# A streaming conformer layer: weight buffers told apart by kind, sums of weights made ahead, and a changed order of FFN products

## The chip, the cores and the metric

The kernel runs on one core of one Trainium2 chip. A core has five engines that work side by side, each through its own instructions in order: TensorE (PE, matrix products, its weight loads shown apart as PEld), VectorE (DVE), ScalarE (ACT), GpSimd (POOL) and SyncE (SP), which here does nothing but ask for DMA transfers. The metric is the device time of one execution in microseconds (us), lower is better. Three runs of the kernel before took 3102.14, 3109.66 and 3117.72 us.

## The reference

One layer over 2048 prompt frames and 64 new sample frames, width 1024, all in float32. Cut to what is computed:

```python
mod = jax.nn.silu(c) @ p['w_ada'] + p['b_ada']            # w_ada 1024 x 6144
sh1, sc1, gt1, sh2, sc2, gt2 = split(mod, 6)
h = rms_norm(x, p['norm1_g']) * (1 + sc1) + sh1
z = h @ p['w_in']                                         # 1024 x 4608
glu_a, glu_b, q, k, v, g_conv, g_attn = split(z)
u = glu_a * sigmoid(glu_b)
conv_out = silu(layer_norm(causal_depthwise_conv31(u) + b_dw)) @ p['w_conv_out']   # 512 x 1024
attn_out = band_attention(rms_norm(q), rms_norm(k), v, rel_bias) @ p['w_attn_out'] # 512 x 1024
merged = sigmoid(g_conv) * conv_out + sigmoid(g_attn) * attn_out
x = x + gt1 * (merged @ p['w_o'])                         # 1024 x 1024
h2 = rms_norm(x, p['norm2_g']) * (1 + sc2) + sh2
gate, up = split(h2 @ p['w_ffn_in'], 2)                   # 1024 x 5632
x = x + gt2 * ((silu(gate) * up) @ p['w_ffn_out'])        # 2816 x 1024
```

Outputs are the new x and the conv, key and value states. There are two modulation vectors, one for the prompt and one for the sample.

## The kernel before, in words

**Precision.** Every matrix operand is split into a rounded high part and a low remainder (`hi` by an ACT copy, `lo` by a subtraction on DVE or POOL), and a product is three matmuls, hi*hi, hi*lo, lo*hi (`mm3`, line 517).

**Stages.** The 2112 frames go in four blocks through the input projections, the convolution and the attention (up to about 1242 us), whose results are kept in DRAM. Then three blocks (`CBLOCKS`, 704, 640 and 768 frames) each go through the merge (`merge`, products with `ca` weights in column tiles ct), the output projection (`wo`), the residual and second norm (`residual`), and the FFN. The FFN multiplies its 2x2 blocks of input columns and frame halves in a seven-product scheme: with h2 cut into b11, b21 (first half of the frames) and b12, b22, there are frame operands t1 to t4, and weight sums s1 to s4 of the gate and up columns. For each of the 22 column tiles f, `up` (line 1643) runs the products s2*t2, s3*t3, s1*t1, a12*b21, a11*b11, a22*t4, s4*b22 into PSUM banks y, z, x and ny, with DVE and ACT steps between them; u (`u2`) and v are copies of partial results. `down` (line 1689) multiplies the hidden part by the output weights (`fo`) every second f. For the first five f (`EARLY`) the a11 and a12 products of the next block are done before the second half of the residual is finished (lines 1722 to 1736); W.hold keeps the `up` weights back until the residual's rows are done, since the sums and those rows share one tag (`ws`, four slots).

**Weights.** `Weights` (line 216) walks one list of keys (`weight_order`). Raw weights are loaded by SP into a ring of three slots `wst`, in the order of the list; `split` makes hi and lo in a ring of five slots each (`whi`, `wlo`), and the next key is split when a slot comes free. Weights used again are stored split in DRAM and loaded from there into whi and wlo. The modulation's slabs (`mod`, 512 KB of w_ada each, raw) stand in the same list and take `whi` slots. For the first use of an `up` key, `operand` has POOL make all four sums s1 to s4 of one f at once, when a key that needs one is split, and stores them to DRAM for the later blocks.

**Order.** The program's order is written by generators that are stepped on against a model of each engine's load (`Stream`): `stream.at(t, f)` calls f once PE's modelled time reaches t, and a `yield t` holds a generator until then. `TURN_LAG` is added to the time at which the normalised q and k rows (`kn`) are turned by PE (line 841). SP issues its DMAs in order, so one that waits for its data holds those behind it.

## Time and profile before

| what | us |
|---|---|
| median of three runs | 3109.66 |
| the profiled execution, whole | 3108.83 |
| its span, first to last instruction | 3106.9 |
| PE busy | 2976.5 |
| DVE busy | 1783.5 |
| ACT busy | 1180.2 |
| POOL busy | 1021.2 |

The profile is of one execution. A row of grouped instructions gives the engine, the operation, what it writes and reads by the program's names (out<-in), shapes and count, then the busy time and the mean duration in ns, then the idle time of the engine just before, with what ended it. In a row of waits stand the waiting engine and what it writes, then what it waited for, the total, the count and the longest. In a row of time order stand the start, the duration, the engine, what it did, and in brackets the idle time before it. SPq stands for SP's queue. Line 98 is the helper through which every compute instruction is recorded, so groups are told apart by their names. The granted clock is the share of full speed at which PE ran.

### The profile page before, as it was taken

The numbers are of one execution on the slowest core, as the hardware profiler recorded it, in microseconds if no ns is written. First come the engines' busy times: TensorE is split into PE (matmuls) and PEld (weight loads), VectorE is DVE, ScalarE is ACT, GpSimd is POOL, SyncE is SP. The second block draws the span as 40 slices with busy tenths as digits, with TensorE's granted clock in tenths as the row PEclk, the third lists the DMA queues.
The fourth block names the chain that finished last, engine by engine and source line by source line (L and its number), as shares of the span: only waits on it lengthen the run. The fifth ranks groups of instructions, "written<-read, shape, count | busy, mean of one in ns | idle before, by whom it ended". The sixth has DMA issues, their size and how long they took to land. (4 is left out here: it accounts for less than half of the span.)

```text
span 3106.9 us, 44447 instructions
## 1 busy us (share of the span) xinstructions
PE 2976.5 (96%) x16403; PEld 2641.3 (85%) x16403; DVE 1783.5 (57%) x3438; ACT 1180.2 (38%) x2105; POOL 1021.2 (33%) x638
## 2 busy tenths in 40 slices
PE   7999889999999999999999999999999999999999
PEld 4789767887788788898888897889999988999998
DVE  5798677777877895464333335554444555344344
ACT  3324432452245257354333342443333244332331
POOL 1201210111011102328767773434445342343331
PEclk9999999999999999999999999999999999999999
DMA  8889788887887788776445459654444965334434
GB/s 294 272 282 302 242 262 295 256 269 261 282 278 252 259 267 261 239 251 213 141 162 172 147 192 320 227 195 153 150 150 138 321 223 193 127 112 135 136 112 163
DMA packets 480238, 676.26 MB, mean 218 GB/s; under 512 B 37820, under 2 KB 316176, under 8 KB 480021
## 3 DMA queue, kind: packets, MB, share of 16 engines
q1 hardware_dynamic: 467669, 656.04, 64.4%
q10 hardware_dynamic: 12160, 17.35, 1.6%
q8 instruction: 129, 2.11, 0.3%
q14 instruction: 88, 0.72, 0.1%
q0 software_dynamic: 192, 0.04, 0.0%
HBM read 501.70 MB, written 171.61 MB: 217 GB/s over the span
## 5 line engine op out<-in xcount | busy, mean ns | idle before, releaser
L98 POOL TENSOR_TENSOR wlo<-wst,whi 128x1024 fp32r<-128x1024 f32 (+1 forms) x296 | 643.1, 2183 | 821.7 <-ACT whi L98 728.5
L98 ACT ACTIVATE whi<-wst 128x1024 fp32r<-128x1024 f32 (+1 forms) x361 | 354.1, 988 | 581.3 <-PE pd L98 235.0
L98 PE MATMUL ps<-t,whi 128*128 128x352 f32 (+2 forms) x2112 | 511.2, 326 | 22.4 <-ACT u L98 14.8
L98 PE MATMUL pd<-whi,hid 128*128 128x512 f32 (+1 forms) x1496 | 466.2, 390 | 0.0
L98 PEld LDWEIGHTS ps<-t,whi 128*128 128x128 f32 x2112 | 371.5, 190 | 28.4 <-ACT u L98 17.2
L98 PE MATMUL ps<-b,whi 128*128 128x352 f32 (+2 forms) x1584 | 387.7, 327 | 7.6 <-ACT early L98 5.8
L98 DVE SCALAR_TENSOR_TENSOR y<-u,wd,y 128x512 f32<-128x512 f32 (+1 forms) x480 | 371.2, 777 | 6.9
L98 PE MATMUL ps<-hh,whi 128*128 128x512 f32 (+2 forms) x992 | 364.4, 367 | 5.7 <-DVE part_l L98 2.6
L98 PE MATMUL ps<-hl,whi 128*128 128x512 f32 (+2 forms) x992 | 348.7, 351 | 0.0
L98 PE MATMUL ps<-hh,wlo 128*128 128x512 f32 (+2 forms) x992 | 347.5, 351 | 0.2 <-DVE wlo L98 0.2
L98 PE MATMUL ps<-t,wlo 128*128 128x352 f32 (+2 forms) x1056 | 342.6, 325 | 0.0
L98 PEld LDWEIGHTS pd<-whi,hid 128*128 128x128 f32 (+1 forms) x1496 | 276.1, 185 | 62.9 <-issue 0.2
L98 DVE TENSOR_TENSOR acc<-acc,pd 128x512 f32<-128x512 f32 (+1 forms) x272 | 186.8, 687 | 201.1 <-PE pd L98 201.1
L98 PE MATMUL pd<-wlo,hid 128*128 128x512 f32 (+1 forms) x748 | 291.7, 390 | 0.7 <-DMA wlo<-w_dfo_l 0.7
L98 PEld LDWEIGHTS ps<-b,whi 128*128 128x128 f32 x1584 | 278.6, 190 | 12.0 <-ACT early L98 7.7
L98 PE MATMUL ps<-b,wlo 128*128 128x352 f32 (+2 forms) x792 | 257.6, 325 | 0.0
L98 POOL TENSOR_TENSOR r<-t,mhalf 128x1 f32<-128x1 f32 (+3 forms) x68 | 84.4, 1242 | 472.9 <-DVE t L98 434.2
L98 PEld LDWEIGHTS ps<-hh,whi 128*128 128x128 f32 x992 | 190.7, 192 | 24.6 <-issue 5.1
L98 PEld LDWEIGHTS ps<-hh,wlo 128*128 128x128 f32 x992 | 189.4, 191 | 23.3 <-DVE wlo L98 0.5
L98 PEld LDWEIGHTS ps<-hl,whi 128*128 128x128 f32 x992 | 190.3, 192 | 16.1 <-issue 1.7
L98 PEld LDWEIGHTS ps<-t,wlo 128*128 128x128 f32 x1056 | 200.8, 190 | 0.0
L98 PE MATMUL ps<-cin,whi 128*128 128x384 f32 (+2 forms) x768 | 185.1, 327 | 7.3 <-DVE t L98 4.5
(198 smaller groups left out, 5102.0 us busy)
## 6 DMA issues: line engine op xcount, KB each, us to landing
wst<-sum_d SPq DMA_DIRECT2D x176, 256.0 KB, 2.9
whi<-w_din_h SPq DMA_DIRECT2D x72, 512.0 KB, 6.3
wlo<-w_din_l SPq DMA_DIRECT2D x72, 512.0 KB, 6.9
wst<-in_w_ffn_in SPq DMA_DIRECT2D x112, 256.0 KB, 3.3
wst<-in_w_ffn_in SPq DMA_DIRECT2D x49, 512.0 KB, 4.5
wmod<-in_w_ada SPq DMA_DIRECT2D x48, 512.0 KB, 7.4
wst<-in_w_o SPq DMA_DIRECT2D x48, 512.0 KB, 4.8
sum_d<-ws SPq DMA_DIRECT2D x88, 256.0 KB, 2.0
```

The lines of the kernel that those rows point to most:

```text
L98: return f(*args, **kw)
```

## The change

1. **Modulation.** The slabs leave the list of `Weights`. A class `Slabs` gives them four slots `wmod` of their own; the next slab is asked for when PE is done with one. The room comes from `dynamic_dma_scratch_size=1024` (it reserves less room for transfers), and the six small vector loads that POOL's queue issued go to ACT's.
2. **Raw weights.** From the merge on there are two more tags: `wfo`, two slots for raw `fo` weights, and `wup`, one more slot for all others. A slot is given back when its last user is done (`drop`), for raw FFN columns after each single sum. In `Weights.__init__` the first three raw weights are loaded and split at once.
3. **Sums.** `operand` makes sums one at a time, as many as are asked for; `presum` makes those of the next key as soon as its raw columns are modelled to have landed. Each is stored to DRAM on its own.
4. **`fi` weights** (the first five column tiles) are split in two halves, lo on POOL, not DVE.
5. **FFN order.** In `up`, a22 stands ahead of a11; for f = 0, s3 ahead of s2; v is copied from z right after s3, and the former f's second hidden half is split ahead of u's copy. The first five a11 and a12 products are interleaved over f, and more of them stand behind the last turn.
6. **Second chunk's inputs** of the first merge are loaded at its third column tile, not ahead of the merge.
7. **Last products.** Only the first tile of `down`'s last pass goes weight by weight; the others finish one half before the other starts. For the very last tile acc*gt + x1 is made ahead of the matmuls.
8. **Lags.** TURN_LAG 1500 to 2500, also added to the modulation's column steps; output stores 4000 later (`OUT_LAG`).

The diff, cut to its core:

```diff
-TURN_LAG = 1500.0
+TURN_LAG = 2500.0
+OUT_LAG = 4000.0
...
+class Slabs:
+    def fill(self):
+        while len(self.ready) < min(len(self.keys), self.freed + self.held):
+            (src,), a, b = self.source(self.keys[len(self.ready)])
+            w = self.pool.tile([P, a, b], F32, tag="wmod", name="wmod", bufs=self.held)
+            self.sync.dma_start(w, src)
+            self.ready.append(w)
...
+    def done(self):
+        self.given += 1
+        self.stream.at(self.stream.when("pe"), lambda n=self.given: self.free(n), True)
...
+        self.extra = {"wup": 1, "wfo": 2}
+        self.tags = {"fo": ("wfo",), "": ("wst", "wup")}
...
+        self.load_on("")
...
+    def last_phase(self, sum_pool, sum_d):
+        self.sum_pool, self.sum_d = sum_pool, sum_d
+        for kind, tag in (("fo", "wfo"), ("", "wup")):
+            self.room[tag] = self.extra[tag]
+            self.load_on(kind)
...
     def operand(self, f, op):
...
-        if f not in self.sums:
-            t = [self.sum_pool.tile([P, 4, P], F32, tag="ws", name="ws", bufs=4) for _ in range(4)]
...
+        made = self.sums.setdefault(f, [])
+        while len(made) < int(op[1]):
+            j = len(made)
+            t = self.sum_pool.tile([P, 4, P], F32, tag="ws", name="ws", bufs=4)
...
+            self.gps.tensor_tensor(t, x, y, e)
+            made.append(t)
+            for c in self.parts_of(f, f"s{j + 1}"):
+                self.drop(self.raws[c], "pool")
+            self.stream.at(
+                self.stream.when("pool"), lambda j=j, t=t: self.sync.dma_start(self.sum_d[f][j], t), True
+            )
+        return made[int(op[1]) - 1]
+
+    def presum(self):
+
+        i = len(self.ready)
+        if i in self.first and all(self.landed.get(j, 1e18) <= self.stream.load["pe"] for j in self.need[i]):
+            for f, op in self.keys[i][1:]:
+                if op[0] == "s":
+                    self.operand(f, op)
...
-        e, name = (self.dve, "dve") if key[0] in ("in", "qkv", "fi") or key[0] == "wo" and key[1] % 2 else (self.gps, "pool")
+        e, name = (self.dve, "dve") if key[0] in ("in", "qkv") or key[0] == "wo" and key[1] % 2 else (self.gps, "pool")
...
-            parts = [(slice(0, shape[1]), self.loaded[its[0]])]
+            n = 4 if key[0] == "fi" else shape[1]
+            parts = [(slice(j, j + n), self.loaded[its[0]][0][:, j : j + n]) for j in range(0, shape[1], n)]
...
-    ops = ["s2", "s3", "s1"] + ["a12"] * (f >= EARLY) + ["a11"] * (EARLY <= f + 1 < NF) + ["a22", "s4"]
+    ops = (["s2", "s3", "s1"] if f else ["s3", "s2", "s1"]) + ["a12"] * (f >= EARLY) + ["a22"] + ["a11"] * (EARLY <= f + 1 < NF) + ["s4"]
...
-            nc.gpsimd.dma_start(r1[o : o + a.shape[0]], a)
+            nc.scalar.dma_start(r1[o : o + a.shape[0]], a)
...
-                stream.when("dve"), lambda pa=pa, R=R, c6=c6, half=half: mod_columns(pa[:, 2 * P :], R, c6, 4 * half, 2)
+                stream.when("dve") + TURN_LAG, lambda pa=pa, R=R, c6=c6, half=half: mod_columns(pa[:, 2 * P :], R, c6, 4 * half, 2)
...
+    M = Slabs(nc.sync, wa, stream, list(mod_order()), source, 4)
+    M.fill()
...
             g = ahead.pop(0)
+            if ct == 2 and load:
+                load()
...
             step(y, "s2", "t2", f < EARLY, False)
-            u2 = piece("t1", "u2")[:, :half]
-            keep = (lambda dst: plus(dst, y, s1)) if f < EARLY else (lambda dst: copy(dst, y))
-            keep(u2)
             if late:
                 hidden(*late.pop())
-            z = bank("y")
-            step(z, "s3", "t3", True, False)
+            u2 = piece("t1", "u2")[:, :half]
+            keep = (lambda dst, ps: plus(dst, ps, s1)) if f < EARLY else copy
+            keep(u2, y)
+            if f:
+                z = bank("y")
+                step(z, "s3", "t3", True, False)
+            v = half_piece(1, "v")[:, :half]
+            keep(v, z)
             between()
             step(y, "s1", "t1", False, False)
-            v = half_piece(1, "v")[:, :half]
-            keep(v)
-            plus(v, z, v)
+            plus(v, y, v)
...
+                final = last and hi == T and i == len(tiles) - 1
+                x1 = [x1s[q // 3][:n, q % 3] for q in (2 * i, 2 * i + 1)] if last else None
+                if final:
+                    for j in range(2):
+                        dst = acc[i][:n, 512 * j : 512 * j + 512]
+                        dve.tensor_tensor(dst, dst, gt[:n, 512 * j : 512 * j + 512], ALU.mult)
+                        dve.tensor_tensor(dst, dst, x1[j], ALU.add)
...
-        for f in range(EARLY):
-            if f == EARLY - 2:
-                turns.drain()
-                W.hold = False
-                W.fill()
...
+        for step, f in ((first, 0), (first, 1), (second, 0), (first, 2), (second, 1)):
+            step(f)
+        while hs["columns"]:
+            turns.step(turns.gens[0])
+        W.hold = False
+        W.presum()
         turns.drain()
+        for step, f in ((first, 3), (first, 4), (second, 2), (second, 3), (second, 4)):
+            step(f)
+            W.fill()
...
-    nc = bacc.Bacc("TRN2", target_bir_lowering=False, num_devices=1)
+    nc = bacc.Bacc("TRN2", target_bir_lowering=False, num_devices=1, dynamic_dma_scratch_size=1024)
```

## Prediction

> **What bounds the kernel now.** I read the page first, then the mean granted clock, then busy time by stage, then who TensorE (PE) waited for, then the stretches in which its clock was halved.

> ```profile
> span 3106.9 us, 44447 instructions
> ...
> PE 2976.5 (96%) x16403; PEld 2641.3 (85%) x16403; DVE 1783.5 (57%) x3438; ACT 1180.2 (38%) x2105; POOL 1021.2 (33%) x638
> ```

> ```profile
> core 0: 3106.9 us, clock 0.987
> ```

> PE is busy for 2976.5 of 3106.9 us, so all its idle time is 130 us; a mean clock of 0.987 costs up to 0.013 x 3106.9 = 40 us more. No edit shortens a matmul, so 170 us is the ceiling. The stages share it unevenly (stretch, its length, then busy us of PE, PEld, DVE, ACT, POOL, granted clock, DMA share, GB/s):

> ```profile
> 33.40:1242.00 1208.60, 1147.25 (x6425) 965.68 (x6424) 930.23 (x1916) 494.57 (x955) 149.79 (x134) 0.98 0.84 271
> ...
> 1414.00:1884.00 470.00, 455.10 (x2470) 415.81 (x2471) 185.67 (x323) 162.44 (x305) 326.50 (x240) 0.99 0.53 180
> ...
> 2051.00:2429.00 378.00, 377.89 (x2266) 354.86 (x2264) 153.85 (x282) 131.09 (x213) 163.24 (x69) 1.00 0.48 158
> ...
> 2616.00:3100.00 484.00, 484.00 (x2531) 451.50 (x2531) 202.31 (x338) 141.48 (x219) 163.93 (x70) 1.00 0.41 133
> ```

> Projections and attention (to 1242) lose 61 us of PE. The FFN of block 0 loses 15; the FFNs of blocks 1 and 2 lose nothing, so there an edit can only cost. The waits of PE (total us, times, longest) name what could go:

> ```profile
> PE pt L98 <- DVE kn L98: 16.1, 9, 3.4
> PE ps L98 <- ACT u L98: 14.8, 8, 2.1
> ...
> PE ps L98 <- ACT t L98: 7.6, 2, 4.3
> PE ps L98 <- DMA whi<-w_dqkv_h: 7.1, 3, 2.6
> PE ps L98 <- ACT early L98: 5.8, 3, 3.3
> ...
> PE ps L98 <- DVE t L98: 4.5, 1, 4.5
> PE ps L98 <- POOL wlo L98: 3.9, 4, 1.7
> PE pa L98 <- DVE R L98: 3.5, 5, 1.0
> ...
> PE ps L98 <- DMA whi<-w_din_h: 2.4, 1, 2.4
> ```

> Behind several of them the granted clock (third number from the end) falls to a half:

> ```profile
> 408.80:415.60 6.80, 5.71 (x18) 4.66 (x18) 5.97 (x18) 1.85 (x8) 0.00 (x0) 0.50 1.01 368
> 463.40:470.20 6.80, 5.53 (x18) 4.78 (x19) 4.71 (x11) 2.40 (x6) 0.00 (x0) 0.50 1.02 402
> ...
> 1262.20:1265.50 3.30, 3.09 (x11) 3.09 (x12) 2.74 (x7) 1.52 (x3) 0.00 (x0) 0.50 0.63 189
> 1402.10:1408.90 6.80, 6.05 (x21) 6.05 (x22) 4.93 (x9) 3.73 (x9) 6.72 (x7) 0.50 0.89 302
> 1412.40:1419.10 6.70, 5.03 (x17) 5.03 (x18) 2.69 (x4) 2.20 (x4) 6.64 (x6) 0.50 0.73 240
> 1552.30:1555.70 3.40, 3.40 (x14) 3.40 (x13) 0.28 (x1) 0.64 (x2) 2.38 (x1) 0.50 0.38 154
> 1736.70:1740.00 3.30, 3.30 (x13) 3.30 (x12) 0.52 (x1) 0.46 (x1) 1.91 (x1) 0.50 0.57 230
> ...
> 2043.90:2050.60 6.70, 5.49 (x20) 5.50 (x21) 4.99 (x9) 1.68 (x3) 2.14 (x1) 0.50 0.52 157
> ```

> I price such a stretch at half its PE busy time.

> **The change part by part** (gain in us, in brackets the two ends).

> *Modulation slabs leave the ring: 11 (0 to 15.1).* Four slabs of a modulation step hold four of the five hi slots, so the next weights are asked for in one burst when they come free:

> ```profile
> 460.84 0.53 SPq L314 DMA_DIRECT2D whi<-w_dqkv_h  x1
> ...
> 466.96 0.32 SPq L314 DMA_DIRECT2D wlo<-w_din_l  x1
> ```

> Ten loads in 6.4 us, while PE waits. With slots of their own they are asked for one by one, earlier. Waits 7.1 + 2.4 = 9.5; clock (5.71 + 5.53)/2 = 5.6. The DMA share of 1.01 and 1.02 there says that part of it is a queue for bandwidth, and bytes don't change, so I take 7 + 4.

> *TURN_LAG 1500 to 2500: 8 (-3.5 to 12.5).* Nine waits on kn, each at most 1 us shorter since the transposes stand 1 us later in PE's order: at most 9, I take 6, as some are under 1 us. The modulation columns move by 2.5 us, past the five waits on R: of 3.5, I take 2. The splits of kn and their stores to q_d and k_d move back with the transposes, behind other loads on SP's queue; the attention that reads them is put into the order only after the v product. The product's bank (pa) is held longer; if this comes back as waits of the same size, it is -3.5.

> *The start: -1 (-3.7 to 0).* The first three raw weights are now split as soon as they are asked for; until now their slots were full of slabs. They are issued late,

> ```profile
> 10.94 2.79 SPq L270 DMA_DIRECT2D wst<-in_w_in  x3
> ```

> and their three subtractions (1.24 us each on DVE, row below) can stand ahead of the modulation's small DVE steps. The six vector loads that go from POOL's queue to ACT's are costed at nothing, for ACT's first work waits for x there:

> ```profile
> 4.67 0.63 ACT L98 ACTIVATE junk<-x_t 64x512 f32<-64x512 f32 x1 [1.28 <-DMA x_t<-in_x_sample]
> ```

> Beyond those 1.28 us of cover each adds its issue time ahead of the squares.

> *Second chunk's inputs asked for at the third column tile: 2.5 (-2 to 6).* The wait on t (4.5) is for gate columns queued behind 3.1 MB (4 x 128 x 4 x 384 x 4 B); with the clock 4.5 + 3.09/2 = 6.0. The same bytes now stand in front of a later gate column, so I take under half; at worst a wait of half the size appears as well as the old one.

> *First FFN products interleaved, s3 ahead of s2: 14 (4 to 21.7).* One half product is 12 matmuls:

> ```profile
> 1827.71 35.08 PE ps L98 x216
> ```

> 12 x 35.08/216 = 1.95 us. After the last turn five of them stand ahead of f=0's first T product, not four, and t3 is split before t2: of the 7.6 for t I take 5.5. Between first and second of one f stands another half product: the three waits on early (5.8, longest 3.3) leave 1.4, so 4.4. Clock: (6.05 + 5.03 + 5.49)/2 = 8.3, half of it 4.1.

> *Sums ahead of need, raw and last weights in their own buffers: 14 (0 to 18.1).* In block 0's FFN:

> ```profile
> 1503.30 0.63 ACT L98 ACTIVATE whi<-ws 128x512 fp32r<-128x512 f32 x1 [3.32 <-POOL ws L98]
> ...
> 1505.41 0.46 ACT L98 ACTIVATE u<-ps 128x352 f32<-128x352 f32 x1
> ```

> ACT stands in its queue for a sum that POOL only just makes; the copy of u is behind it, and PE waits for the copy, eight times 1.85 us. Once sums are made when their raws land, ACT finds them ready. 14.8 + (3.40 + 3.30)/2 = 18.1; I take 12 + 2. The four stores of a block's sums are asked for one at a time instead of together, so SP's queue only gets shorter bursts. POOL is busy 326.5 of 470 us there and gets no more work.

> *A fourth raw slot at the merges: 2.5 (-2 to 3.9)* of the 3.9 that PE waits for POOL's lo parts.

> *Lo parts of the first five slabs from DVE to POOL, in halves: -1 (-4.4 to 1.2).* DVE sheds 5 x 1.24 us, POOL gets 10 x 1.30 = 13 us, with the rows' rsqrt behind them in its queue:

> ```profile
> L98 DVE TENSOR_TENSOR wlo<-wst,whi 128x1024 fp32r<-128x1024 f32 x65 | 80.0, 1236 | 79.4 <-ACT whi L98 76.2 <-DMA gk<-in_k_norm_g 3.0
> ...
> L98 POOL TENSOR_TENSOR wlo<-wst,whi 128x512 fp32r<-128x512 f32 x60 | 76.6, 1295 | 12.2 <-ACT whi L98 12.2
> ```

> ```profile
> 1408.97 1.55 DVE L98 TENSOR_TENSOR b<-xn,b 128x512 fp32r<-128x512 f32 x1
> ...
> 2043.08 0.74 DVE L98 TENSOR_TENSOR b<-xn,b 128x512 fp32r<-128x512 f32 x1
> ```

> The same step took 1.55 us in block 0, where POOL worked beside it, and 0.74 in block 1: 0.81 us lost where the two meet. Ten pieces, ten meetings at most: 8.1 us of DVE against 6.2 shed, and some of the rsqrt's delay, but only the last pieces lie near the drain that PE waits for. I take 1. [...]

> *Tail: 1.8 (1 to 2.5).*

> ```profile
> 3100.18 0.39 PE L98 MATMUL pd<-whi,hid 128*128 128x512 f32 x1
> ```

> ```profile
> 3101.21 1.29 DVE L98 TENSOR_TENSOR pd<-pd,gt 128x512 f32<-128x512 f32 x2
> 3102.41 1.28 DVE L98 TENSOR_TENSOR acc<-pd,x 128x512 f32<-128x512 f32 x2
> ```

> The last matmul ends at 3100.57, DVE at 3103.69: 3.1 us. Afterwards only one half's two steps (0.65 + 0.64) follow it.

> *Fourth product ahead of a11, v copied from z, hidden ahead of u's copy, OUT_LAG: 0.* Counts stay; the output stores move 4 us back on SP's queue, past weight loads that gain by it, and nothing reads them; in blocks 1 and 2 PE has no idle time to give. Their cover is ACT (141 of 484 us busy); what it costs without that is the slower rival.

> Sum: 11 + 8 - 1 + 2.5 + 14 + 14 + 2.5 - 1 + 1.8 = 51.8. The profiled execution took 3108.83 (span 3106.9); the median of the runs, 3109.66, is 0.8 above it. 3109.7 - 51.8 = **3058 us**.

> **The rivals.**
> - *Bandwidth, not the ring.* The bursts go, but the same bytes at a share near 1 keep PE waiting, at the slabs and at the gate columns: 11 + 2.5 less, 3071. For it the two shares over 1; against it the stage's mean of 0.84.
> - *The sums stay late.* Their tiles keep a ring of four, which the residual's x rows share, so the change may not do what it says: POOL waits for a slot where it waited for raws. 14 less, 3072. Against: POOL is idle for 143 us of that stage.
> - *Both, and the new order of first products waits elsewhere* (a further 14 less): 3058 + 13.5 + 14 + 14 = 3099, no measurable change.
> - *All covered:* every upper end without the start's loss, 15.1 + 12.5 + 6 + 21.7 + 18.1 + 3.9 + 1.2 + 2.5 = 81: 3029.
> - *Slower: ACT's queue in the products.* Splitting the former hidden half now stands ahead of u's copy; for an odd f only one half product (1.95 us) lies between, and s1 waits for the copy. If each of the 33 pairs of f (11 in each of three blocks) then waits as the eight do now, 14.8/8 + 3.35/8 = 2.27, that is 75 us lost, and block 0's 14 not won: 3109.7 + 75 - 37.8 = 3147. It decides from 37.8/33 = 1.15 us a pair. For it: a weight's copy of 0.63 us or a wait can land in that spot. Against: ACT is idle for 70% of those stages.
> - *The clock stretches have other causes than these waits.* Then the waits go and the halves stay: 4 + 4.1 + 2 + some 1 of the sum, 3069. Against it:

> ```profile
> 1551.58 0.59 PE L98 MATMUL ps<-t,whi 128*128 128x352 f32 x2 [1.93 <-ACT u L98]
> ```

> A wait of 1.93 us ends 0.7 us ahead of a half-clock stretch; six others of the eight have none. [...]

> **How the numbers follow.** Forecast 0.47, bandwidth 0.13, late sums 0.11, all covered 0.10, clock 0.04: 0.85 on the faster side. No change 0.08, slower 0.07. A measurement of this kernel tells about 0.5% (15.5 us) from no change. The range runs from 3029 (all covered) to 3099 (no change), which leaves out the slower case, part of the other two: 3029 to 3099. The likeliest case's own range, its terms a quarter off, is 3045 to 3071.

> **What would show it.** Slabs: no wait of PE on w_dqkv or w_din, clock 1.00 near 410 and 465. Lag: the kn waits' total under 11 us. Sums: no PE wait on u between 1400 and 1850, ACT not released by POOL ws. First products: t and early together under 5 us. Tail: under 2 us from the last matmul to DVE's end. Wrong if PE's busy share in the FFNs of blocks 1 and 2 leaves 100%, above all by waits on u; or if the idle time at the slabs stays with DMA named.

## The result and the profile after

The changed kernel took 3077.64 us (median of four runs, 3072.38 to 3079.68), the kernel before 3109.04 beside it: ratio 0.9895, 95% interval 0.9867 to 0.9923. It is 31 us faster, where 52 were forecast. The profiled execution, the fastest of the four, spans 3070.6 us, 36.3 less than before. From the page of the changed kernel, whose mean clock was 0.986:

```profile
span 3070.6 us, 44482 instructions
...
PE 2960.8 (96%) x16403; PEld 2634.3 (86%) x16403; DVE 1781.8 (58%) x3435; ACT 1179.6 (38%) x2110; POOL 1027.6 (33%) x642
```

PE's idle time is 109.8 us (130 before). To see where the time went I cut both traces at the first product of each block's merge, as here for the changed kernel, in order of time (start, duration, engine, what it did, in brackets the idle time before it):

```profile
1223.43 0.56 PE L99 MATMUL ps<-cin,whi 128*128 128x320 f32 x2 [1.41 <-DVE o_p L99]
...
1874.92 0.41 PE L99 MATMUL ps<-cin,whi 128*128 128x256 f32 x2
...
2423.60 0.52 PE L99 MATMUL ps<-cin,whi 128*128 128x384 f32 x2
```

| us | projections, attention | block 0 | block 1 | block 2 to the end |
|---|---|---|---|---|
| before | 1243.5 | 651.8 | 557.3 | 654.3 |
| after | 1223.4 | 651.5 | 548.7 | 647.0 |
| gain | 20.1 | 0.3 | 8.6 | 7.3 |

Block 0 stood out: the largest part of the forecast lay there, and it gained nothing. The waits of PE (total us, times, longest), the whole kernel after:

```profile
PE pd L99 <- ACT whi L99: 16.4, 1, 16.4
PE pt L99 <- DVE kn L99: 11.2, 3, 5.0
...
PE ps L99 <- DVE t L99: 9.9, 5, 6.1
PE ptp L99 <- DVE pr L99: 7.5, 8, 2.9
...
PE ps L99 <- ACT t L99: 3.3, 4, 1.4
...
PE ps L99 <- ACT early L99: 1.8, 2, 1.6
...
PE pa L99 <- DVE R L99: 1.6, 2, 0.8
```

The waits on u (14.8), on w_dqkv_h (7.1) and on w_din_h (2.4) are gone; those on kn, t from ACT and early are smaller. A wait of 16.4 us is new. In order of time it stands in block 0's last `down`:

```profile
1814.80 10.07 SPq L1866 DMA_DIRECT2D x<-x_d  x12
...
1831.75 2.82 SPq L981 DMA_DIRECT2D cin<-o_d  x2
1834.66 1.73 SPq L328 DMA_DIRECT2D wfo<-in_w_ffn_out  x1
...
1845.67 1.06 ACT L99 ACTIVATE whi<-wfo 128x1024 fp32r<-128x1024 f32 x1 [21.27 <-DMA wfo<-in_w_ffn_out]
1846.78 1.12 PE L99 MATMUL pd<-whi,hid 128*64 128x512 f32 x2 [16.35 <-ACT whi L99]
1849.21 0.69 PE L99 MATMUL pd<-wlo,hid 128*64 128x512 f32 x1 [1.32 <-POOL wlo L99]
```

The last pass needs four output weights and `wfo` has two slots. The fourth load is asked for at 1834.66, behind all the loads for later work on SP's queue, and PE waits. In the kernel before, the same load went out ahead of them:

```profile
1852.65 0.35 SPq L270 DMA_DIRECT2D wst<-in_w_ffn_out  x1
...
1854.84 11.97 SPq L1750 DMA_DIRECT2D x<-x_d  x12
```

What was a ring in the list's order had become two queues of loads: once each kind had slots of its own, the next merge's weights were asked for from 1793 on, ahead of the last two output weights:

```profile
1793.26 0.38 SPq L328 DMA_DIRECT2D wst<-in_w_conv_out  x1
...
1812.11 0.35 SPq L328 DMA_DIRECT2D wfo<-in_w_ffn_out  x1
```

### The profile page after: what moved, and what is told of

It is laid out like the page before. It is cut to its first block, busy times and chain, and to the rows that moved or that the text cites. A ratio compares the mean times of both kernels' runs of the same rounds, so it can differ in the third digit from the quotient of the medians.

```text
span 3070.6 us, 44482 instructions
## 1 busy us (share of the span) xinstructions
PE 2960.8 (96%) x16403; PEld 2634.3 (86%) x16403; DVE 1781.8 (58%) x3435; ACT 1179.6 (38%) x2110; POOL 1027.6 (33%) x642
## 5 line engine op out<-in xcount | busy, mean ns | idle before, releaser
L99 POOL TENSOR_TENSOR wlo<-wst,whi 128x1024 fp32r<-128x1024 f32 (+1 forms) x215 | 458.7, 2142 | 607.8 <-ACT whi L99 555.6
L99 PE MATMUL pd<-whi,hid 128*128 128x512 f32 (+1 forms) x1496 | 467.9, 391 | 16.4 <-ACT whi L99 16.4
L99 ACT ACTIVATE whi<-wst 128x1024 fp32r<-128x1024 f32 (+1 forms) x268 | 258.9, 975 | 433.2 <-PE pd L99 180.8
L99 PE MATMUL ps<-b,whi 128*128 128x352 f32 (+2 forms) x1584 | 381.4, 324 | 2.9 <-ACT early L99 1.8
L99 POOL TENSOR_TENSOR wlo<-wup,whi 128x1024 fp32r<-128x1024 f32 (+1 forms) x69 | 146.0, 2116 | 149.2 <-ACT whi L99 128.8
```

Of the source, the lines that this page charges most:

```text
L99: return f(*args, **kw)
```

## The experiments

Twelve runs, each beside the kernel before on the same chip (its median 3107.9 beside the first four, 3105.4 beside the next four, 3107.3 beside the three after them, 3107.4 beside the last). V stands for the changed kernel with the output weights first, the first experiment; the seven rows that begin with it are edits of it. The cuts of all of them, in us:

| run | median | ratio, interval | proj., att. | block 0 | block 1 | block 2 |
|---|---|---|---|---|---|---|
| output weights first (V) | 3052.7 | 0.9822 (0.9803, 0.9842) | 1227.4 | 631.5 | 545.8 | 647.8 |
| sums not ahead | 3080.3 | 0.9909 (0.9893, 0.9925) | 1230.1 | 655.8 | 545.9 | 647.0 |
| old first products | 3076.2 | 0.9897 (0.9879, 0.9916) | 1221.9 | 652.8 | 548.0 | 649.1 |
| before + slabs alone | 3089.0 | 0.9939 (0.9919, 0.9959) | 1222.8 | 650.3 | 555.9 | 654.0 |
| V, lag 1500 | 3049.3 | 0.9815 (0.9795, 0.9835) | 1230.0 | 629.6 | 544.5 | 647.8 |
| V, no fourth raw slot | 3087.2 | 0.9938 (0.9923, 0.9953) | 1228.3 | 656.1 | 546.6 | 649.9 |
| V, old order in up | 3055.3 | 0.9838 (0.9823, 0.9852) | 1228.4 | 634.1 | 547.4 | 647.5 |
| V, old order, late sums | 3057.3 | 0.9836 (0.982, 0.9853) | 1235.1 | 634.1 | 546.5 | 647.7 |
| V, mixed inputs early | 3060.4 | 0.9851 (0.9835, 0.9867) | 1226.7 | 636.8 | 544.8 | 647.2 |
| V, wfo filled later | 3055.3 | 0.9833 (0.9818, 0.9848) | 1228.9 | 628.3 | 547.6 | 647.0 |
| V, fi lo on DVE | 3058.9 | 0.9842 (0.9827, 0.9856) | 1232.2 | 633.2 | 545.4 | 647.3 |
| six shared slots | 3056.0 | 0.9829 (0.9807, 0.985) | 1230.0 | 631.6 | 545.7 | 647.7 |

In the first stage even the runs that edit nothing there, with the changed kernel's own 1223.4, lie between 1221.9 and 1235.1, so a difference under some 10 us says nothing in that column or in a single median. The columns of the blocks repeat within 2 to 3 us, and the small terms are read there.

**Output weights first.** All four are fetched at the start of the last pass:

```diff
         drain()
+        fos = [W.get(("fo", f)) for f in range(NF - 4, NF)]
         gt2 = {which: gt_row(1, which) ...
...
-            ws = [W.get(("fo", f)) for f in fs]
+            ws = fos if last else [W.get(("fo", f)) for f in fs]
```

> The changed kernel, but the four output weights of the last pass of each block's down are fetched ahead of the gt2 rows, the x1 rows and the next block's inputs. Theory: block 0 lost 16.4 us (PE waits for ACT whi, released by the load of the fourth raw fo weight, asked for at 1834.66 behind 24 transfers on SP's queue), 1.3 us for its lo part and about half of the 5.8 us that the clock stays halved afterwards; all of it goes: the PE wait on ACT whi under 3 us, the time 3077.6 - 20 = 3057 (3050 to 3062). Rival, the transfers of that moment are limited by bandwidth and the wait only moves to the gate columns or the mixed inputs of the next merge: 3072 to 3080. Second rival, the fourth raw weight can't start before POOL's split of the second gives its slot back: the wait keeps about a third, 3065.

Block 0 became 20.0 us shorter and the median 25 us lower. Of PE's waits between 1800 and 1870 in this trace one is left, and the load stands ahead of the x rows:

```profile
PE pd L99 <- POOL wlo L99: 1.5, 1, 1.5
```

```profile
1818.98 0.33 SPq L328 DMA_DIRECT2D wfo<-in_w_ffn_out  x1
...
1819.88 10.88 SPq L1867 DMA_DIRECT2D x<-x_d  x12
```

The wait did not reappear in the next merge (block 1 is 2.9 us shorter, not longer), so both rivals fall. The 20 us by which the changed kernel missed its forecast are the size of this one wait.

**Sums not ahead.** `presum` never makes a sum:

```diff
-        if i in self.first and all(self.landed.get(j, 1e18) <= self.stream.load["pe"] for j in self.need[i]):
+        if False and i in self.first and all(self.landed.get(j, 1e18) <= self.stream.load["pe"] for j in self.need[i]):
```

> The changed kernel without presum: sums are made one by one when a split asks for them, as late as before, while raw and last weights keep their own buffers. Theory (the forecast's term of 14 us in block 0's FFN is real and only covered up by the new wait of 16.4 us there): PE waits on ACT u come back, 10 to 15 us in all between 1400 and 1850, time 3077.6 + 12 = 3090. Rival, the waits on u went because hidden and u's copy changed places or because the raws land earlier: no wait on u, 3074 to 3081.

The rival held: no wait on u came back, block 0 is 4.3 us longer. ACT's waits for sums between 1400 and 1820, here and in the kernel before:

```profile
ACT whi L99 <- POOL ws L99: 7.0, 3, 3.3
```

```profile
ACT whi L98 <- POOL ws L98: 82.1, 28, 5.9
```

**Old first products.**

```diff
-    ops = (["s2", "s3", "s1"] if f else ["s3", "s2", "s1"]) + ...
+    ops = ["s2", "s3", "s1"] + ...
...
-        for step, f in ((first, 0), (first, 1), (second, 0), (first, 2), (second, 1)):
+        for step, f in ((first, 0), (second, 0), (first, 1), (second, 1), (first, 2), (second, 2)):
...
-        for step, f in ((first, 3), (first, 4), (second, 2), (second, 3), (second, 4)):
+        for step, f in ((first, 3), (second, 3), (first, 4), (second, 4)):
```

> The changed kernel with the old order of the first FFN products (both products of f one after the other, s2 ahead of s3 for f = 0; the turns drained after three f, two behind them). Theory (term of 14 us): PE waits on ACT t and early come back from 5.1 us to 11 to 14 us and with them half-clock stretches at two merges; time 3077.6 + 12 = 3090 (3084 to 3094), the three merges 10 to 15 us longer in sum. Rival, the merges gained from the fourth raw slot or the later mixed inputs instead: 3075 to 3081.

The rival held. Against the changed kernel the blocks differ by +1.3, -0.7 and +2.1: about 3 us for a term of 14, no more than these columns differ by in any case. The waits on early came back, those on t from ACT did not:

```profile
PE ps L99 <- ACT early L99: 8.1, 4, 2.5
...
PE ps L99 <- ACT t L99: 3.3, 2, 1.7
```

**The kernel before with the slabs alone.** `Slabs` and `mod_order` as in the change, the vector loads on ACT's queue and the smaller scratch, and of `weight_order`:

```diff
-    mods = iter([("mod", *half, i) for half in MOD_HALVES for i in range(4)])
...
+    yield from (("qkv", 0, k) for k in range(4))
     for b, stage in ORDER:
...
-        yield from (next(mods) for _ in range(4 * MODS.get((b, stage), 0)))
```

> The kernel before, with the modulation slabs alone taken out of the weights' ring into four slots of their own (and the vector loads on ACT's queue, the smaller transfer scratch that pays for it). Theory (term 1 of 11 us): no PE wait on w_dqkv or w_din, projections and attention end 8 to 14 us earlier than in the kernel before (1243.5), time 3109 - 11 = 3098. Rival, the later turns made the gain of that stage (20.1 us in the changed kernel) and the loads are held by bandwidth: stage shorter by under 4 us, 3105 to 3110.

The first stage is 20.7 us shorter, all that the changed kernel has there, and the whole is 18.9 us faster. PE's idle time makes up 11 us of the 20.7. In the two stretches that had run at half clock:

```profile
408.80:415.60 6.80, 6.80 (x33) 5.26 (x32) 5.87 (x16) 2.11 (x7) 0.00 (x0) 1.00 0.89 246
463.40:470.20 6.80, 6.75 (x34) 5.24 (x32) 6.71 (x14) 2.07 (x5) 0.00 (x0) 1.00 0.99 320
```

PE is busy throughout at full clock beside a DMA share of 0.89 and 0.99. Fewer bytes move in these stretches (246 and 320 GB/s, 368 and 402 before), since part of them was asked for earlier. The stage as a whole moves its bytes in less time (274 GB/s against 271): their number was not the limit, the order in which they were asked for was.

Part of the gain is lost again a little later. Between 470 and 520 PE waited 2.3 us for the softmax's row values (`sm`) in the kernel before; here it waits 8.0 us, 7.1 of them while DVE runs twelve steps of the depthwise convolution ahead of the step that makes them:

```profile
PE sc L98 <- DVE sm L98: 8.0, 2, 7.1
```

```profile
497.97 9.41 DVE L98 SCALAR_TENSOR_TENSOR y<-u,wd,y 128x512 f32<-128x512 f32 x12
```

The changed kernel has this wait too (6.7 us), and 13.7 us at half clock with it, where the kernel before has 3.4 (its clock in the same stretch is 0.88, PE busy for 11.18):

```profile
500.90:514.60 13.70, 7.05 (x22) 5.74 (x23) 12.30 (x28) 2.77 (x6) 0.00 (x0) 0.50 0.87 321
```

**Lag back at 1500 (V).**

```diff
-TURN_LAG = 2500.0
+TURN_LAG = 1500.0
```

> The version with the output weights first (3052.7 us), with TURN_LAG back at 1500 for the turns and the modulation's columns. Theory from the slabs-alone run (the whole 20 us of the projections and attention come from the slabs): the lag is worth 0 there, time 3050 to 3056, waits on kn 11 to 13 us as in the slabs-alone run. Rival, the forecast's term of 8 us: kn waits back at 16 us and R at 3.5 us, time 3059 to 3063.

The lag is worth nothing that these runs can tell. What the shorter lag adds on kn the longer one adds on pr (this run, then V):

```profile
PE pt L99 <- DVE kn L99: 13.7, 6, 4.1
...
PE ptp L99 <- DVE pr L99: 5.3, 5, 2.1
```

```profile
PE pt L99 <- DVE kn L99: 11.1, 3, 5.0
...
PE ptp L99 <- DVE pr L99: 8.0, 9, 2.7
```

**No fourth raw slot (V).**

```diff
-        self.extra = {"wup": 1, "wfo": 2}
+        self.extra = {"wup": 0, "wfo": 2}
```

> The version with the output weights first (3052.7 us), without the extra slot wup: three raw slots for all weights but the output ones. Theory: the second and third merges gained 11.6 and 5.5 us, more than the 2.5 us put down for the fourth slot, and the old order of first products did not give it back; so the fourth slot made it, waits on POOL wlo return at the merges, and the time is 3062 to 3068, FFN of block 0 included. Rival, the slots are not short once the output weights have their own: 3051 to 3056, no POOL wlo wait over 1 us.

Slower than V by 34.5 us in the medians and 28.4 in the spans, more than twice the expected: 24.6 of it in block 0, little at the later merges (+0.8 and +2.1). PE's waits of the whole run and ACT's between 1400 and 1820:

```profile
PE ps L99 <- ACT s L99: 14.4, 7, 2.1
```

```profile
ACT whi L99 <- POOL ws L99: 61.5, 27, 6.4
```

That is the old picture with another name, s (the copy of the a11 product) in place of u: ACT stands in its queue for a sum that POOL makes late, since a raw column landed late. POOL's waits for raw columns in that stretch, here and in the kernel before (the changed kernel has none):

```profile
POOL ws L99 <- DMA wst<-in_w_ffn_in: 14.5, 10, 3.6
```

```profile
POOL ws L98 <- DMA wst<-in_w_ffn_in: 7.8, 10, 1.3
```

`presum` is still in, and it can't make a sum of a column that hasn't landed.

**Old order in `up`, and the same with late sums (V).**

```diff
...
-            if late:
-                hidden(*late.pop())
             u2 = piece("t1", "u2")[:, :half]
             keep = (lambda dst, ps: plus(dst, ps, s1)) if f < EARLY else copy
             keep(u2, y)
+            if late:
+                hidden(*late.pop())
...
-            v = half_piece(1, "v")[:, :half]
-            keep(v, z)
             between()
             step(y, "s1", "t1", False, False)
-            plus(v, y, v)
+            v = half_piece(1, "v")[:, :half]
+            keep(v, y)
+            plus(v, z, v)
...
-            step(z, "a22", "t4", False, True)
-            plus(z, z, u2)
-            dve.tensor_tensor(z, z, c1, ALU.mult)
             if EARLY <= f + 1 < NF:
...
                 copy(begun[f + 1][1], ny)
+            step(z, "a22", "t4", False, True)
+            plus(z, z, u2)
+            dve.tensor_tensor(z, z, c1, ALU.mult)
```

> The version with the output weights first (3052.7 us), with the old order inside up (u copied ahead of the former hidden half, v copied from y, a11 ahead of a22). Theory (forecast: this part is worth 0, as the sums ahead already keep ACT free): no PE wait on u, time 3050 to 3056. Rival, the new order alone removed the waits on u, since they also stayed away when the sums were not made ahead: u waits of 10 to 15 us back in block 0, time 3064 to 3069. Third, the new order costs ACT time in blocks 1 and 2 (the forecast's slower rival): 3046 to 3050.

> The version with the output weights first (3052.7 us), with the old order inside up and no sums ahead: raw and last weights still have their own buffers. Theory (order and sums ahead each suffice alone, buffers do not): PE waits on u of 10 to 15 us are back in block 0 and the time is 3065 to 3071. Rival, own buffers suffice (raws land earlier, so POOL's sums are ready although made on demand): no u waits, 3052 to 3057.

Neither brought a wait on u back. Block 0 is 2.6 us longer in both, blocks 1 and 2 differ by at most 1.6. So the buffers suffice, with the sums made one at a time, which all these runs keep. The order is worth 2.6 us; early sums are worth nothing beside the old order, and 4.3 us in the run without them above.

**Mixed inputs early, wfo filled later, fi lo on DVE (V).** In this order:

```diff
-    srcs = [src]
+    srcs = [src, load_mixed(*c1, 1)]
...
```

```diff
-        for kind, tag in (("fo", "wfo"), ("", "wup")):
-            self.room[tag] = self.extra[tag]
-            self.load_on(kind)
+        self.room.update(self.extra)
+        self.load_on("")
...
+            if ct == 5 and load:
+                W.load_on("fo")
```

```diff
-        e, name = (self.dve, "dve") if key[0] in ("in", "qkv") or ...
+        e, name = (self.dve, "dve") if key[0] in ("in", "qkv", "fi") or ...
-            n = 4 if key[0] == "fi" else shape[1]
+            n = shape[1]
```

> The version with the output weights first (3052.7 us), with the second chunk's inputs loaded ahead of the first merge again. Theory: the gate columns that PE waits for at the third column tile (6.2 us, then 6.8 us at half clock) now stand behind the first loads of the new buffers wfo and wup (1.5 MB asked for at 1235 to 1237), not behind the mixed inputs, so the later load was a loss of its gain only by that; with the mixed inputs in front again the wait grows to 8 to 12 us and the time is 3055 to 3059. Rival, moving the mixed inputs gained nothing and cost nothing: wait 4 to 7 us, 3049 to 3055.

> The version with the output weights first (3052.7 us), with the first two loads into wfo asked for at the sixth column tile of the first merge, not at its start. Theory: they stand ahead of the gate columns on SP's queue and in bandwidth; the PE wait on DVE t of 6.2 us near 1240 falls under 3 us and the half clock behind it goes, time 3052.7 - 7 = 3046 (3043 to 3049). Rival, the gate columns wait for the first chunk's own stores (c_d) or for wup and the mixed inputs: wait still 4 us or more, 3050 to 3055.

> The version with the output weights first (3052.7 us), with the lo parts of the first five column tiles on DVE again, in one piece each. Theory: block 0's waits on t and early stayed away under the old order of first products, so moving 5 x 1.24 us off DVE ahead of the first T product made that gain, not the order: PE waits on ACT t and early of 4 us or more are back at about 1390, time 3056 to 3060. Rival, both are worth nothing alone because each covers the other: 3050 to 3055. Third, the forecast: POOL's pieces cost 1 us, so it is 3051 to 3052.

The wait at the third column tile of the first merge was to go. In V it is 6.2 us, with

```profile
1235.21 0.81 SPq L328 DMA_DIRECT2D wfo<-in_w_ffn_out  x2
1236.07 0.43 SPq L328 DMA_DIRECT2D wup<-in_w_conv_out  x1
1236.54 0.87 SPq L328 DMA_DIRECT2D wup<-in_w_attn_out  x1
1237.46 1.85 SPq L973 DMA_DIRECT2D tg<-g_d  x3
...
1244.42 0.90 PE L99 MATMUL ps<-cin,whi 128*128 128x320 f32 x2 [6.22 <-DVE t L99]
```

Four loads, which fill the three new slots, stand ahead of the gate columns. PE's waits between 1220 and 1420 with the mixed inputs early, and with the `wfo` loads later:

```profile
PE ps L99 <- DVE t L99: 8.4, 3, 6.2
```

```profile
PE ps L99 <- DVE t L99: 5.1, 3, 2.9
```

With the mixed inputs in front the longest wait stays 6.2 where 8 to 12 were expected, so that theory falls; yet block 0 is 5.3 us longer and the median, 3060.4, lies above both expected ranges. Of the 5.3, PE waits 1.5 us for a lo part and 1.6 us more for t from ACT than in V; the rest is open. With the `wfo` loads later it is 2.9, as expected, and block 0 3.2 us shorter, but the first stage and block 1 give 1.5 and 1.8 us back and the median is not the expected 3046: the mechanism is seen, its worth is about 3 us at most.

With the lo parts on DVE block 0 is 1.7 us longer, and PE waits more for t in that stretch, 1.8 us in V and 4.7 here:

```profile
PE ps L99 <- ACT t L99: 4.7, 3, 1.9
```

The direction is that of the theory. The median, 3058.9, lies in its range of 3056 to 3060, but 4.8 us of the difference stand in the first stage, which this edit does not touch; what block 0 shows is less than the theory's 4 us and within the spread of its column.

**Six shared slots.** An edit of the changed kernel; the output weights are not moved.

```diff
-        return "fo" if key[0] == "fo" else ""
+        return ""
...
-        self.extra = {"wup": 1, "wfo": 2}
-        self.tags = {"fo": ("wfo",), "": ("wst", "wup")}
+        self.extra = {"wup": 3}
+        self.tags = {"": ("wst", "wup")}
```

> The changed kernel with the raw slots not told apart by kind: the three further slots (one wup, two wfo) all serve the common list, in the list's order, so that output weights and others share six slots; nothing is fetched out of order and the output weights are not moved ahead of the x1 rows. Theory (number of raw slots made the gain of block 0's FFN, separation by kind made the new wait, since the merge's weights took the free slots 20 us ahead of the fourth output weight): PE wait on ACT whi in the last pass gone, waits on u and s stay away, time 3050 to 3056. Rival, the separate buffers made the gain, as the output weights no longer stand between the columns: u or s waits of 5 us or more back in block 0, time 3062 to 3070. Third, the wait comes from the x1 rows' place on SP's queue whatever the slots: it stays at 10 us or more, time 3068 to 3078.

The theory held: 3056.0 us, block 0 as in V, and between 1400 and 1870 PE waits for nothing but t, 2.2 us from ACT and 0.3 from DVE:

```profile
PE ps L99 <- ACT t L99: 2.2, 1, 2.2
```

The room made the gain in block 0; keeping the kinds apart made the loss.

## Why the prediction was right and wrong

The direction was right and the time 20 us too low: 3077.6 us lies in the whole range (3029 to 3099), but outside the 3045 to 3071 of the likeliest case. It comes near the rivals of bandwidth and of late sums (3071, 3072) without the mechanism of either: PE no longer waits on w_dqkv_h, on w_din_h or on u. Without the new wait the kernel takes 3052.7 us, 55 under its kernel before, against a sum of 51.8. The terms that make up those 55 are not the ones of the sum, so that this comes so close is luck.

- **The step that failed: that buffers of their own could cost nothing.** The term for sums and own buffers had 0 as its lower end, and no rival had a loss there. In that term only the sums' stores were followed on SP's queue; that a list with two rings is no longer fetched in its order, and that two slots serve a pass of four weights, was not looked at. That cost block 0 20 us, and it was undone by fetching four weights earlier, or by one shared list.
- **Sums ahead and own buffers (14).** The size was low and the reason wrong. The wait on u went as forecast, but through the fourth raw slot (24.6 us of block 0 without it), not through `presum` (4.3 in the changed kernel, nothing on top of the old order). "POOL is idle for 143 us" was a right reading: its sums were late since the raws were.
- **Slabs (11).** Undersized, as far as this column can tell: 20.7 us in the first stage of the slabs-alone run, and 15.1, the upper end, if one takes the mean of that stage over the eleven other versions with the slabs and the new lag (1228.4). I cut the waits and the clock from 15.1 because the DMA share was 1.01 and 1.02. The slabs-alone run shows no wait in these stretches, so nothing had to be taken off for bandwidth, and for the slabs that rival falls. What the term left out is that PE then meets a longer wait 35 us later, the one on sm.
- **The clock as its own cause.** The time that this rival names came out about half so. In the first stage the two stretches shown went, but others came: the stage has 51.2 us at half clock in the changed kernel and 47.8 before, summed over windows of 0.4 us, and PE's work in them fell only from 42.6 to 38.9 us. The longest of the new ones, 13.7 us from 500.9 on, begins with the wait of 5.8 us on sm, 0.9 us behind one of 3.5 us on kk; what the others follow is open, so a cause other than waits is not shown.
- **TURN_LAG (8).** Nothing that the runs can tell: kn fell from 16.1 to 11.2 (under 11 was the sign named) and waits on pr rose from 3.5 to 7.5. R fell from 3.5 to 1.6, but does so with the slabs alone too.
- **Start (-1).** Not tried alone.
- **First products (14).** About 3 us. The waits on t and early were priced at most of their size (5.5 of 7.6, 4.4 of 5.8), but under the old order t from ACT was already 3.3 us in place of 7.6. So other edits had shed it; the lo parts on POOL may be one of them, which 1.7 us can't show. With the new order t and early come to 5.1 us, where under 5 was the sign named.
- **fi lo parts (-1).** The sign was wrong, if anything: with them on DVE block 0 is 1.7 us longer. In the row of 0.74 us POOL is at work too, but its piece ends 0.2 us after that step starts (2043.27). A meeting can cost more than the 0.81 us priced: in the changed kernel the same step takes 0.68 us at 1382.08, where POOL is idle, and 1.91 us at 2016.05, where a POOL piece of 2.40 us runs until 2017.41.
- **Second chunk's inputs (2.5).** The wait grew from 4.5 to 6.1 us instead of falling, for the first loads of the new buffers stand in the place that the mixed inputs left; with two of them later it is 2.9. Undoing the move made block 0 5.3 us longer, in one trace.
- **Fourth slot at the merges (2.5).** Block 1 gained 8.6 us. Before, SP asked for its merge's weights while it ran, and PE waited for their lo parts:

```profile
1904.09 0.39 PE L98 MATMUL ps<-cin,wlo 128*128 128x256 f32 x1 [1.70 <-POOL wlo L98]
1904.25 0.44 SPq L270 DMA_DIRECT2D wst<-in_w_conv_out  x1
```

  Now they are asked for from 1793 on, 80 us ahead of the merge: the same early request that pushed the output weight back. The gain stayed without the fourth slot (546.6), so that slot is not its cause. It stayed as well with six shared slots (545.7), where the output weights hold slots again and the merge's weights are asked for from 1811 on, 50 us ahead. So more raw slots in either form fit it; no run takes them all away, nor the later output stores (`OUT_LAG`), and the cause is not shown.
- **Tail (1.8).** As forecast: the last matmul ends at 3065.98, DVE at 3067.44, 1.5 us against 3.1.

```profile
3065.59 0.39 PE L99 MATMUL pd<-whi,hid 128*128 128x512 f32 x1
...
3066.75 0.69 DVE L99 TENSOR_TENSOR acc<-pd,acc 128x512 f32<-128x512 f32 x1
```

- **The slower rival (ACT's queue in `up`)** had nothing in it: PE is busy for 482.86 of 483 us in block 2's FFN, and the old order changes blocks 1 and 2 by at most 1.6 us.

```profile
2583.00:3066.00 483.00, 482.86 (x2524) 450.87 (x2522) 208.36 (x345) 141.19 (x220) 166.45 (x71) 1.00 0.41 134
```

Open: why the lag moves its wait to pr; what block 1 gained by; what `OUT_LAG` and the start are worth, which no run tried alone; and the 3.6 us of block 2 that neither tail nor first products account for (7.3 - 1.6 - 2.1). Open as well is the spread of 13 us in the first stage, between runs that edit nothing there; the mean clock of the whole profiled execution was 0.986 in the run with the shortest (old first products) and 0.984 in the one with the longest (old order, late sums).

## What to carry to other kernels

When one ring of buffers is cut into several, write down the order in which loads now leave and check the one that is needed first against everything that may pass it; room and separation are two edits, and here one slot more gave 24.6 us in block 0 and the separation took 20. A late sum, copy or product can be a late load two steps back, as in block 0: there the cure was a slot, and moving the consumers' order added 2.6 us. A DMA share near 1 beside a waiting engine (1.02 at the slabs, behind ten loads asked for in 6.4 us) was no proof of a bandwidth limit here: in V, PE is busy for 30.51 of 32 us at a share of 1.01, at full clock.

```profile
1826.00:1858.00 32.00, 30.51 (x135) 24.06 (x134) 23.80 (x37) 4.09 (x6) 4.74 (x2) 1.00 1.01 355
```

## What the runs showed of the hardware

The long wait shows how the clock falls and comes back. PE's last matmul ends at 1830.43, and the next starts at 1846.78. Busy time, granted clock, DMA share and GB/s in the changed kernel:

```profile
1830.50:1835.40 4.90, 0.00 (x0) 0.00 (x0) 0.00 (x0) 0.00 (x0) 0.00 (x0) 1.00 1.09 353
1835.50:1846.70 11.20, 0.00 (x0) 0.00 (x0) 0.00 (x0) 1.03 (x2) 0.00 (x0) 0.50 1.06 388
1846.80:1852.50 5.70, 4.38 (x10) 2.56 (x11) 2.10 (x4) 0.88 (x1) 4.68 (x2) 0.50 0.93 381
```
